# A decoder trunk on one core: a new address raster for the operand pools, the second scale matrix on VectorE, and the last probabilities product placed earlier

## The chip, the core and the metric

The kernel runs on one core of a Trainium2 chip, as one launch. The metric is the device time of that launch in microseconds (us). The kernel before takes 2453.76 us (median of three runs, 2452.49 to 2454.29). Differences of 0.2% and less, about 4.9 us here, cannot be told from no change.

## What is computed

Two decoder layers over 1024 tokens of width 1024, all in float32. The layers differ in their mixer; the rest is the same:

```python
h = x
for layer in range(2):
    hn = rmsnorm(h, g_mix[layer])
    # layer 0: gated convolution + gMLP gating; layer 1: latent attention (8 heads) + mLSTM (4 heads)
    mix = even_mixer(hn, ...) if layer % 2 == 0 else odd_mixer(hn, positions, ...)
    h = h + mix                                  # mix ends in a 1024 x 1024 output projection
    h = h + swiglu(rmsnorm(h, g_ffn[layer]), w_gate[layer], w_up[layer], w_down[layer])   # D_FF = 2816
    gate = sigmoid(rmsnorm(h, g_ple[layer]) @ w_ple_gate[layer])
    h = h + gate * (p[layer] @ w_ple_proj[layer])
```

Attention is causal softmax over blocks of 128 queries; each head's output is the product of its probabilities with V, and the heads are concatenated before the output projection.

## The kernel before

**Products.** The work is held transposed: tiles of 128 partitions by 512 columns, two token halves `n` of 512 tokens, eight feature blocks `k` of 128. A float32 operand is kept as two fp32r tiles, a high part made on ScalarE (`split`, L146) and the remainder made on VectorE (L147), with the letters `h` and `l` in their names (`xch`, `xcl`; `hu`, `lu`). One product of 128x128 by 128x512 is three matmuls, high by high, low by high and high by low (`mm3`, L189 to L191). In the rows a matmul reads `out<-moving,stationary`: `p<-xch,hu` streams `xch` past the weights `hu`. The stationary operand of the next matmul is loaded (PEld) while the matmul before it streams.

**Where tiles lie.** Pools are stacked in each partition's memory in the order in which they are opened: constants; `opB` (32 slots of 2 KB); `w`, which holds six tiles with the tag `raw` (weights as they come from memory, 2 KB each), eight `whi` and eight `wlo` (the split weights); `tmp` (working tiles, some of them 2056 bytes or a few bytes long); and last `opA` (the slots from number 32 up), which the attention's own pools replace during attention. A slot below 32 is in `opB`, one from 32 up in `opA`. With the sizes of the program, `opB`, `raw`, `whi` and `wlo` all begin at 832 bytes past a multiple of 2048 (`opB` at byte 19264, `whi` at 97088, `wlo` ends at 129856), and `opA` begins at byte 151488, which is 1984 past a multiple of 2048. Taken modulo 256 that is 64 for the first group and 192 for `opA`. "Raster" below means this remainder.

**Which products use which pool.** Layer 0's input projection reads the normalised input from the `x0` tiles, which lie in `opA` (slots 32 to 63); its weights are the `w` tiles. SwiGLU's gate and up projections are done by a seven-product scheme on quarters of the operands: for each of 22 column units and each layer, 7 products of 4 operand pairs, each pair one `mm3`. The operand tiles of products 1 and 2 (`xb`) and 4 lie in `opB`; those of the rest (`xc`) are placed as they are made, in the order 6, 7, 5, 4, 3, by

```python
free = iter(list(range(32, 54)) + list(range(16, 32)) + [54, 55])
```

so that products 6 and 7 lie in `opA` wholly, of product 5 three pairs in four, and of product 3 one pair in four: 12 of the 28 pairs. The gate projection at the layer's end (`ppg`) keeps the first token half in `opB` and the second in `opA`; its projection of `p` (`ppj`) has its tokens `pT` in `opA`, and at the end of layer 1 its weights `wj` too.

**Row scales.** `bcast_prep` splits a row vector of scales in two and puts each part on the diagonals of a 128x512 matrix, `dg`; `bcast` multiplies both with a matrix of ones (`Rb`, L298 and L299) so that the scales stand in all partitions, and ScalarE copies the sum out. This happens ten times in the program.

**The end of attention.** A loop over 64 pairs of head and query block transposes probabilities (`PT`, L1875), has ScalarE copy them out (`PTs`, L1877) and multiplies them with V (`O<-V,PTs`, L1833) one step later: `lag` holds the product that is still to be done. After a head's last product `head_done` divides by the row sums (`yp`, L1815), and after a pair of heads `pair_out` transposes the pair's output for a token half (`yaT`, L1824) and splits it (`y1h`, `y1l`), from where it is an operand of the output projection. The two `pair_out` calls of the last pair wait in `todo`. Behind the loop the output projection is begun: two output blocks `ot`, each of seven operand pairs (21 matmuls `po`); the eighth pair is the one that the last heads make. The engines run their instructions in the order in which the program issues them; a scheduler of the compiler moves a few neighbours.

Of the kernel before, what the change touches and what calls it, by code (L numbers as in the profile page):

```python
# [11 lines left out]
F32 = mybir.dt.float32  # L12
# [9 lines left out]
P = 128  # L22
# [4 lines left out]
HT = 512  # L27
# [12 lines left out]
RAW = 6  # L40
# [6 lines left out]
class Build:  # L47
# [59 lines left out]

    def w_part(self, srcs, kt, cols, name, gcol, slots=None):
        nc = self.nc
        raw = self.wp.tile([P, kt, cols], F32, tag="raw", name=self.name(f"r{name}"), bufs=RAW)  # L110
        o = 0
        for s in srcs:
            w = s.shape[1]
            nc.sync.dma_start(raw[:, :, o : o + w], s.rearrange("(k p) c -> p k c", p=P))
            o += w
        if gcol is not None and kt > 1:
            g = self.vec[:, gcol : gcol + kt].unsqueeze(2).to_broadcast([P, kt, cols])
            nc.gpsimd.tensor_tensor(out=raw, in0=raw, in1=g, op=ALU.mult)
        if slots:
            hi, lo = (  # L120
                self.slot(i, name=f"u{name}").rearrange("p (k c) -> p k c", k=kt) for i in slots
            )
        else:
            hi = self.wp.tile([P, kt, cols], F32R, tag="whi", name=self.name(f"h{name}"), bufs=8)
            lo = self.wp.tile([P, kt, cols], F32R, tag="wlo", name=self.name(f"l{name}"), bufs=8)
        if gcol is not None and kt == 1:
            self.split_scaled(hi, lo, raw, self.vec[:, gcol : gcol + 1])
        else:
            self.split(hi, lo, raw)
        return [(hi[:, k, :], lo[:, k, :]) for k in range(kt)]  # L130
# [23 lines left out]

    def w_quarter(self, w, rows, c, name):

        t = self.wp.tile([P, 4, P], F32, tag="raw", name=self.name(f"r{name}"), bufs=RAW)
        self.nc.sync.dma_start(
            t, w[rows * HT : (rows + 1) * HT, c].rearrange("(k p) c -> p k c", p=P)
        )  # L160
        return t
# [7 lines left out]
    def w_chain(self, w, c0, c1, name, eng):  # L169


        tt = eng.tensor_tensor
        raw = lambda: self.wp.tile([P, 4, P], F32, tag="raw", name=self.name(f"s{name}"), bufs=RAW)
        a11 = self.w_quarter(w, 0, c0, name)
        a21 = self.w_quarter(w, 0, c1, name)
        a22 = self.w_quarter(w, 1, c1, name)
        a12 = self.w_quarter(w, 1, c0, name)
        s1, s2 = raw(), raw()
        tt(out=s1, in0=a21, in1=a22, op=ALU.add)
        tt(out=s2, in0=s1, in1=a11, op=ALU.subtract)  # L180
        tt(out=a21, in0=a11, in1=a21, op=ALU.subtract)
        return {1: a11, 2: a12, 4: a22, 5: s1, 6: s2, 7: a21}
# [95 lines left out]
    def bcast_prep(self, r):  # L278

        nc = self.nc  # L280
        rh = self.tp.tile([P, 4], F32R, tag="rh", name=self.name("rh"), bufs=2)
        rl = self.small("rl", (P, 4))
        nc.vector.tensor_copy(rh, r)
        nc.vector.tensor_tensor(out=rl, in0=r, in1=rh.bitcast(F32), op=ALU.subtract)
        out = []
        for i, x in enumerate((rh.bitcast(F32), rl)):
            d = self.tmp("dg", (P, 4, P), F32R)
            (nc.vector, nc.gpsimd)[i].tensor_tensor(
                out=d, in0=self.ident.unsqueeze(1).to_broadcast([P, 4, P]),
                in1=x.unsqueeze(2).to_broadcast([P, 4, P]), op=ALU.mult,  # L290
            )
            out.append(d.rearrange("p a b -> p (a b)"))
        return out
# [31 lines left out]
def trunk(ctx, tc, x, p, positions, g_mix, g_ffn, g_ple, ev_w_in, ev_w_conv, ev_g_v, ev_w_s,  # L325
          ev_b_s, ev_w_out, od_w_in, od_b_gate, od_g_qa, od_g_kva, od_w_q_up, od_w_kv_up, od_g_q,
          od_g_k, od_g_mh, od_w_out, w_gate, w_up, w_down, w_ple_proj, w_ple_gate, out):
    nc = tc.nc
    B = Build(tc)
    x = x[0]  # L330
# [3 lines left out]
    bp = ctx.enter_context(tc.tile_pool(name="opB", bufs=1))  # L334
    dp = ctx.enter_context(tc.tile_pool(name="dram", bufs=1, space=DRAM))
    B.wp = ctx.enter_context(tc.tile_pool(name="w", bufs=1))
    B.tp = ctx.enter_context(tc.tile_pool(name="tmp", bufs=1))

    def open_ps():
        s = ExitStack()  # L340
# [316 lines left out]
    def ffn_down(l, act_d, h_d, h2_d, X2, st, normed):  # L657
# [6 lines left out]

        def part(fh, ch, f, t=None):
            if t is None:
                t = B.wp.tile([P, HT], F32, tag="raw", name=B.name("rd"), bufs=RAW)
            r = (fh * half + f) * P
            nc.sync.dma_start(t, w_down[l][r : r + P, ch * HT : (ch + 1) * HT])
            return t  # L670
# [163 lines left out]
    def ple_out(l, tok, h2_d, X, r):  # L834

        pT = {}
        for n in range(2):
            pT[n] = make_pT(load_p(l, n) if n else tok, [32 + 4 * n + i for i in range(4)])
        for cg in range(2):
            c = slice(cg * HT, (cg + 1) * HT)  # L840
            grp = B.tm_load(w_ple_gate[l], [(cg * HT, (cg + 1) * HT)], f"pg{cg}")
            hs = {}
            for n in range(2):
                for j in range(4):
                    t = hs[n, j] = B.slot(n * 4 + j + 8 * cg, F32, "h2")
                    nc.sync.dma_start(t, h2_d[n][cg * 4 + j])
            wj = []
            for k in range(2):
                raw = B.wp.tile([P, HT], F32, tag="raw", name=B.name("rpj"), bufs=RAW)
                nc.sync.dma_start(raw, w_ple_proj[l][k * P : (k + 1) * P, c])  # L850
                a = B.slots2(40 + 4 * cg + 2 * k, 41 + 4 * cg + 2 * k, "wj")
                B.split(a[0], a[1], raw)
                wj.append(a)
            for tt in range(NT):
                n, t = tt // 4, slice((tt % 4) * P, (tt % 4 + 1) * P)
                pg = B.tm_mm(grp, X, tt, "ppg")
                pj = B.ps("ppj")
                for k in range(2):
                    a = pT[n][k]
                    B.mm3(pj, (a[0][:, t], a[1][:, t]), wj[k], k == 0, k == 1)  # L860
                ph = B.ps_tr("ph")
                for j in range(4):
                    nc.tensor.transpose(ph[:, j * P : (j + 1) * P], hs[n, j][:, t], ident)
                s = B.tmp("psg")
                nc.scalar.activation(s, pg, AF.Sigmoid, scale=r[n][:, tt % 4 : tt % 4 + 1])
                nc.vector.tensor_tensor(out=s, in0=pj, in1=s, op=ALU.mult)
                nc.vector.tensor_tensor(out=s, in0=ph, in1=s, op=ALU.add)
                nc.sync.dma_start(out[tt * P : (tt + 1) * P, c], s)
# [373 lines left out]
    def up_weights(src, kt, cols, gcol, name):  # L1242
        pairs = []
        half = cols // 2
        for k in range(kt):
# [2 lines left out]
            )  # L1248
            for i in range(2):
                c = slice(i * half, (i + 1) * half)  # L1250
                raw = B.wp.tile([P, half], F32, tag="raw", name=B.name(f"r{name}"), bufs=RAW)
                nc.sync.dma_start(raw, src[k * P : (k + 1) * P, c])
                B.split_scaled(t[0][:, c], t[1][:, c], raw, col(gcol + k))
            pairs.append(t)
# [634 lines left out]
    for ot in range(2):  # L1889
        u = B.w_unit(od_w_out[0][:, ot * P : (ot + 1) * P], KT, P, f"wo{ot}")  # L1890
        po = psum("S", "po", 4)
        for i, k in enumerate(order[:-1]):
            B.mm3(po, u[k], mixT[0][k], i == 0, False)
        begun[0, ot] = u, po
    run_lag()
    for fn in todo:
        fn()
    for _ in mem:
        pass
    at.close()  # L1900
# [44 lines left out]
```

## Time and profile before

| | |
|---|---|
| median of three runs | 2453.76 us |
| the profiled execution | 2453.51 us |
| its span, first to last instruction | 2451.8 us (so 1.7 us lie around it) |
| granted TensorE clock | 0.999 of full speed |
| TensorE matmul (PE) busy | 2413.6 us, 98% |
| VectorE (DVE) busy | 1561.2 us, 64% |
| ScalarE (ACT) busy | 988.2 us, 40% |
| GpSimd (POOL) busy | 679.8 us, 28% |
| DMA, hardware queue | 348.25 MB, 45.3% of 16 engines' span |

A share of busy time is a mean over stages, so each stage has to be read by itself: where PE is busy without a gap, only the rate at which matmuls follow each other can change the time; where another engine is full, PE's rate doesn't matter there.

### The profile page before, as it was taken

To read this page: it belongs to the slowest core of one execution; us is meant where nothing else is said; L and a number is where in the kernel's file an instruction comes from. 1 tells how busy PE (TensorE), PEld (TensorE's weight loads), DVE (VectorE), ACT (ScalarE), POOL (GpSimd) and SP (SyncE) were. 2 spreads that over 40 slices of the span, in tenths; PEclk is the share of its full clock that TensorE was granted. 3 is DMA by queue.
4 is the path that set the end of the run, shared out by engine and by line. 5 is a ranking of instruction groups with operands and counts; after the bars stand their busy time and mean duration, and the time that the engine had idled before them with its cause. 6 is when DMAs were issued, how large, how long until landed. Compare 5 with 4: busy or idle time off the path is not lost.

```text
span 2451.8 us, 33875 instructions
## 1 busy us (share of the span) xinstructions
PE 2413.6 (98%) x11510; PEld 1993.8 (81%) x11510; DVE 1561.2 (64%) x3079; ACT 988.2 (40%) x1877; POOL 679.8 (28%) x678
## 2 busy tenths in 40 slices
PE   7999999999999999999999999999999999999999
PEld 6878887788888888888888788878788888888877
DVE  6864479645556778776785566548855455687731
ACT  5322244233233545444554455635333232454520
POOL 3452121546553000112321132111256556100000
PEclk9999999999999999999999999999999999999999
DMA  4221453433236966553454843154433233886721
GB/s 151 78 86 48 136 169 101 141 99 112 91 108 204 308 226 214 174 173 96 114 154 121 228 112 106 46 168 134 129 120 112 87 111 103 286 281 210 251 97 39
DMA packets 358685, 350.74 MB, mean 143 GB/s; under 512 B 24011, under 2 KB 249648, under 8 KB 358512
## 3 DMA queue, kind: packets, MB, share of 16 engines
q1 hardware_dynamic: 358016, 348.25, 45.3%
q8 instruction: 90, 1.47, 0.2%
q0 software_dynamic: 464, 0.33, 0.1%
q14 instruction: 83, 0.68, 0.1%
q10 hardware_dynamic: 32, 0.01, 0.0%
HBM read 255.18 MB, written 93.32 MB: 142 GB/s over the span
## 4 chain that ended last, share of the span: by engine, by line
PE 52%; DVE 4%; issue 2%; DMA 1%; ACT 1%; POOL 0%; SPq 0%; DVEq 0%; POOLq 0%; ACTq 0%
PE p L190 5%; PE p L189 5%; PE p L191 5%; PE pd L189 3%; PE pd L190 3%; PE pd L191 3%; PE O L1833 2%; PE ppg L191 2%; PE ppg L190 2%; PE ppg L189 2%; PE PT L1875 1%; PE po L189 1%; PE po L190 1%; PE po L191 1%; PE S L1775 1%
## 5 line engine op out<-in xcount | busy, mean ns | idle before, releaser
L189 PE MATMUL pd<-acth,hd 128*128 128x512 f32 x616 | 240.0, 390 | 0.1
L190 PE MATMUL pd<-actl,hd 128*128 128x512 f32 x616 | 239.7, 389 | 0.0
L191 PE MATMUL pd<-acth,ld 128*128 128x512 f32 x616 | 239.7, 389 | 0.0
L189 PE MATMUL p<-xch,hg 128*128 128x512 f32 x440 | 173.1, 394 | 5.3 <-DVE sg L534 2.2
L190 PE MATMUL p<-xcl,hg 128*128 128x512 f32 x440 | 173.1, 393 | 0.2
L189 PE MATMUL p<-xch,hu 128*128 128x512 f32 x440 | 173.0, 393 | 0.0
L191 PE MATMUL p<-xch,lu 128*128 128x512 f32 x440 | 172.9, 393 | 0.0
L191 PE MATMUL p<-xch,lg 128*128 128x512 f32 x440 | 172.9, 393 | 0.0
L190 PE MATMUL p<-xcl,hu 128*128 128x512 f32 x440 | 172.6, 392 | 0.0
L541 POOL TENSOR_TENSOR act<-act,sg 128x512 f32<-128x512 f32 x60 | 90.0, 1499 | 244.1 <-DVE act L534 239.3
L146 ACT CAST hu<-ru 128x512 fp32r<-128x512 f32 x116 | 71.6, 622 | 183.3 <-PE p L190 170.4
L189 PEld LDWEIGHTS pd<-acth,hd 128*128 128x128 f32 x616 | 115.6, 188 | 24.3 <-DVE res L728 0.5
L191 PEld LDWEIGHTS pd<-acth,ld 128*128 128x128 f32 x616 | 115.6, 188 | 24.3
L146 ACT CAST hg<-rg 128x512 fp32r<-128x512 f32 x110 | 68.2, 620 | 165.9 <-PE p L190 135.6
L190 PEld LDWEIGHTS pd<-actl,hd 128*128 128x128 f32 x616 | 115.6, 188 | 23.8
L147 DVE TENSOR_TENSOR lu<-ru,hu 128x512 fp32r<-128x512 f32 x116 | 117.2, 1011 | 14.9 <-ACT hu L146 14.9
L146 ACT CAST hd<-rd 128x512 fp32r<-128x512 f32 x110 | 68.3, 621 | 133.5 <-PE pd L190 82.2
L147 DVE TENSOR_TENSOR actl<-ra,acth 128x512 fp32r<-128x512 f32 x154 | 109.5, 712 | 12.1 <-ACT acth L146 12.0
L259 POOL TENSOR_TENSOR S<-S,sq 128x512 f32<-128x512 f32 x38 | 51.6, 1359 | 219.7 <-ACT sq L257 219.7
L147 DVE TENSOR_TENSOR ld<-rd,hd 128x512 fp32r<-128x512 f32 x110 | 76.9, 699 | 47.6 <-ACT hd L146 47.6
L189 PEld LDWEIGHTS p<-xch,hg 128*128 128x128 f32 x440 | 82.6, 188 | 26.5 <-ACT hg L146 3.0
L146 ACT CAST acth<-ra 128x512 fp32r<-128x512 f32 x154 | 94.7, 616 | 13.1 <-DMA ra<-act 9.3
(561 smaller groups left out, 6615.9 us busy)
## 6 DMA issues: line engine op xcount, KB each, us to landing
ra<-act SPq DMA_DIRECT2D x154, 256.0 KB, 3.7
rd<-in_w_down SPq DMA_DIRECT2D x154, 256.0 KB, 4.0
rg<-in_w_gate SPq DMA_DIRECT2D x100, 256.0 KB, 3.3
ru<-in_w_up SPq DMA_DIRECT2D x100, 256.0 KB, 2.9
act<-act SPq DMA_DIRECT2D x88, 256.0 KB, 2.0
act<-at SPq DMA_DIRECT2D x66, 256.0 KB, 2.0
rpg<-in_w_ple_gate SPq DMA_DIRECT2D x48, 256.0 KB, 3.0
sd<-in_w_down SPq DMA_DIRECT2D x44, 256.0 KB, 4.2
```

The source lines that it names most:

```text
L146: self.nc.scalar.copy(hi, src)
L147: (eng or self.nc.vector).tensor_tensor(out=lo, in0=src, in1=hi.bitcast(F32), op=ALU.subtract)
L189: mm(ps, a[0], b[0], start=first, stop=False, skip_group_check=more)
L190: mm(ps, a[0], b[1], start=False, stop=False, skip_group_check=more)
L191: mm(ps, a[1], b[0], start=False, stop=last, skip_group_check=more)
L259: eng.tensor_tensor(out=st[n], in0=st[n], in1=sq, op=ALU.add)
L541: (nc.vector if last else nc.gpsimd).tensor_tensor(out=t, in0=t, in1=sg[d["i"], key], op=ALU.mult)
L1775: mm(s[:, 0:w], q0, K0[:, c0 : c0 + w], start=True, stop=False)
L1833: nc.tensor.matmul(O[h][:, b * DV : (b + 1) * DV], t[:, j * P : (j + 1) * P], V[h // 2][:, kb, (h % 2) * DV : (h % 2 + 1) * DV], start=kb ...
L1875: nc.tensor.transpose(pt[:, j * P : (j + 1) * P], e[:, j * P : (j + 1) * P], ident)
```

## The change

Three edits:

1. **Pools.** The `raw` tiles leave `w` for a pool of their own, and that pool and `tmp` are placed from the other end of the partition's memory. `opA` then follows directly behind `wlo`.
2. **Scale matrices.** Both `dg` matrices are made on VectorE; before, the second was made on GpSimd.
3. **Last head pair.** `run_lag()`, the last product of probabilities and V, is called ahead of the first output products, and the two `pair_out` calls between the two output blocks.

```diff
@@ w_part, w_quarter, w_chain, part, ple_out, ev: the same edit at each raw tile
-        raw = self.wp.tile([P, kt, cols], F32, tag="raw", name=self.name(f"r{name}"), bufs=RAW)
+        raw = self.rp.tile([P, kt, cols], F32, tag="raw", name=self.name(f"r{name}"), bufs=RAW)
...
@@ bcast_prep
-        for i, x in enumerate((rh.bitcast(F32), rl)):
+        for x in (rh.bitcast(F32), rl):
             d = self.tmp("dg", (P, 4, P), F32R)
-            (nc.vector, nc.gpsimd)[i].tensor_tensor(
+            nc.vector.tensor_tensor(
...
@@ trunk
     B.wp = ctx.enter_context(tc.tile_pool(name="w", bufs=1))
-    B.tp = ctx.enter_context(tc.tile_pool(name="tmp", bufs=1))
+    B.rp = ctx.enter_context(tc.tile_pool(name="raw", bufs=1, side="right"))
+    B.tp = ctx.enter_context(tc.tile_pool(name="tmp", bufs=1, side="right"))
...
@@ end of attention
         po = psum("S", "po", 4)
+        if ot == 0:
+            run_lag()
         for i, k in enumerate(order[:-1]):
             B.mm3(po, u[k], mixT[0][k], i == 0, False)
         begun[0, ot] = u, po
-    run_lag()
-    for fn in todo:
-        fn()
+        if ot == 0:
+            for fn in todo:
+                fn()
```

With the sizes of the program `whi` then begins at byte 84800, `wlo` at 101184 and `opA` at 117568, all 832 past a multiple of 2048, as `opB` still does: every matmul operand of these pools has the remainder 64 modulo 256. The `raw` tiles begin at byte 217056, which is 2016 past a multiple of 2048 and so 32 past a multiple of 64; before they were on a multiple of 64. Which tile is made when, and in which slot, is unchanged. The line numbers behind the edits grow by one to three (L1833 becomes L1834).

On TensorE, at the end of attention, the program before has the last probabilities product behind the second output block, with both transposes of the pair, the eighth operand's products (`y1h_2980`) and nothing else behind it:

```order
L191 MATMUL po_16089<-y1h_2978_13214,lwo_0_3763_16080 128x512
L1833 MATMUL O_15891<-V_15190,PTs_16039 128x64
L1824 MATMUL yaT_16116<-ident,yp_15882 128x128 x4
L189 MATMUL po_16055<-y1h_2980_13216,hwo_0_3755_16045 128x512
L189 MATMUL po_16089<-y1h_2980_13216,hwo_0_3762_16079 128x512
L1824 MATMUL yaT_16123<-ident,yp_15882 128x128 x4
L190 MATMUL po_16055<-y1l_2981_13217,hwo_0_3755_16045 128x512
```

After the change the product stands behind the first output block's third matmul, its first transposes behind that block's last, and the second transposes seven matmuls later:

```order
L191 MATMUL po_16058<-y1h_2982_13221,lwo_4_3759_16055 128x512
L1834 MATMUL O_15894<-V_15193,PTs_16042 128x64
L189 MATMUL po_16058<-y1h_2984_13223,hwo_4_3758_16054 128x512
...
L191 MATMUL po_16058<-y1h_2978_13217,lwo_0_3756_16049 128x512
L1825 MATMUL yaT_16085<-ident,yp_15885 128x128 x4
L189 MATMUL po_16111<-y1h_2982_13221,hwo_4_3768_16107 128x512
...
L189 MATMUL po_16111<-y1h_2986_13225,hwo_4_3768_16107 128x512
L1825 MATMUL yaT_16092<-ident,yp_15885 128x128 x4
```

What moved is `O`, and with it `yp` and `yaT`: 18 matmuls `po` now lie between `O` and the first `yaT`.

On VectorE, at the row scales of layer 0's SwiGLU (`rh` and `rl` are the two parts of the scales, `lu` the low part of a weight tile, `h` the residual that is scaled), before:

```order
L284 TENSOR_TENSOR rl_3272<-rt_3251,rh_3271 128x4
L288 TENSOR_TENSOR dg_3275<-ident,rh_3271 128x512
L147 TENSOR_TENSOR lu_3308<-ru_3305,hu_3307 128x512
L421 SCALAR_TENSOR_TENSOR h_2728<-h_2728,vec,R_3303 128x512
```

and after:

```order
L284 TENSOR_TENSOR rl_3275<-rt_3254,rh_3274 128x4
L288 TENSOR_TENSOR dg_3278<-ident,rh_3274 128x512
L288 TENSOR_TENSOR dg_3280<-ident,rl_3275 128x512
L147 TENSOR_TENSOR lu_3311<-ru_3308,hu_3310 128x512
L422 SCALAR_TENSOR_TENSOR h_2731<-h_2731,vec,R_3306 128x512
```

The second `dg` comes from GpSimd's list, where nothing else changes place, and stands directly behind the first; so it is at all ten places.

## Rows read from the trace of the kernel before

**Rows 1.** The page's first part: busy time of each engine, its share of the span, and its instructions.

```profile
PE 2413.6 (98%) x11510; PEld 1993.8 (81%) x11510; DVE 1561.2 (64%) x3079; ACT 988.2 (40%) x1877; POOL 679.8 (28%) x678
```

**Rows 2.** What TensorE waited for, over the whole span: the line that waited, what it waited for, microseconds in total, how often, the longest.

```profile
PE zv L189 <- ACT x0h L146: 4.0, 1, 4.0
...
PE Rb L299 <- POOL dg L288: 1.5, 4, 0.4
```

**Rows 3.** Busy time of each engine in a stretch of the span (first column, us), with the number of its instructions; the column behind the engines is the granted clock, then the DMA engines' busy share and GB/s. The first stretch is in layer 0's down projection, the second in its input projection; the next two are the beginnings of SwiGLU in layers 0 and 1; the last is layer 1's down projection.

```profile
800.00:900.00 100.00, 100.00 (x442) 82.82 (x442) 75.36 (x123) 51.06 (x92) 0.00 (x0) 1.00 0.82 273
145.00:245.00 100.00, 100.00 (x432) 81.07 (x431) 45.59 (x62) 19.50 (x31) 31.39 (x28) 1.00 0.19 56
361.00:432.00 71.00, 68.50 (x293) 54.13 (x291) 70.06 (x108) 33.72 (x58) 14.05 (x8) 1.00 0.32 100
1690.00:1759.00 69.00, 66.66 (x284) 52.86 (x284) 67.76 (x102) 32.35 (x55) 12.89 (x8) 1.00 0.32 100
2112.00:2325.00 213.00, 212.94 (x946) 176.08 (x945) 166.79 (x275) 102.98 (x183) 6.31 (x4) 1.00 0.77 255
```

**Rows 4.** The timeline of TensorE in SwiGLU of layer 0: start, duration, line, operands. Up to 449.31 the `xch` tiles are those in `opB`, from there on those in `opA`; ten matmuls are left out at each "...".

```profile
446.81 0.39 PE L190 MATMUL p<-xcl,hu 128*128 128x512 f32 x1
...
449.31 0.40 PE L189 MATMUL p<-xch,hu 128*128 128x512 f32 x1
...
451.87 0.39 PE L191 MATMUL p<-xch,lg 128*128 128x512 f32 x1
```

**Rows 5.** The timeline of TensorE at the end of layer 1. In `ppj<-wjh,pTh` both operands lie in `opA`; in `ppg<-hpg,xph` at this place the stationary `xph` is in `opA` and the moving weights in `w`. Three matmuls are left out at the first "...", nine at the last.

```profile
2357.22 0.39 PE L190 MATMUL ppj<-wjl,pTh 128*128 128x512 f32 x1
...
2358.12 0.40 PE L191 MATMUL ppj<-wjh,pTl 128*128 128x512 f32 x1
...
2359.03 0.39 PE L190 MATMUL ppg<-lpg,xph 128*128 128x512 f32 x1
...
2361.35 0.39 PE L191 MATMUL ppg<-hpg,xpl 128*128 128x512 f32 x1
```

**Rows 6.** Groups of TensorE's instructions by line, operands and shape over the whole span: busy time, mean ns of one, idle time before them and who ended it. Each product has its three lines; one line of each is shown.

```profile
L191 PE MATMUL p<-xch,lg 128*128 128x512 f32 x440 | 172.9, 393 | 0.0
...
L189 PE MATMUL ppg<-xph,hpg 128*128 128x512 f32 x128 | 50.4, 394 | 0.0
...
L191 PE MATMUL px<-x0h,lx 128*128 128x512 f32 x64 | 25.3, 395 | 0.0
...
L189 PE MATMUL pu<-x0h,hu 128*128 128x512 f32 x48 | 19.0, 395 | 0.0
...
L191 PE MATMUL zv<-hzva,x0l 128*128 128x512 f32 x32 | 13.2, 412 | 0.0
...
L190 PE MATMUL ppj<-pTl,hpj 128*128 128x512 f32 x32 | 12.7, 397 | 0.0
```

**Rows 7.** The timeline of all engines at the end of attention; a bracket is the idle time of that engine before the instruction and what ended it.

```profile
1589.96 0.27 ACT L1877 COPY PTs<-PT 128x128 f32<-128x128 f32 x1 [0.37 <-PE PT L1875]
1590.11 0.48 PE L191 MATMUL po<-y1h,lwo 128*128 128x512 f32 x1
...
1599.09 0.39 PE L191 MATMUL po<-y1h,lwo 128*128 128x512 f32 x1
...
1599.68 0.69 DVE L1815 TENSOR_TENSOR yp<-O,rr 128x512 f32<-128x512 f32 x1 [1.09 <-PE O L1833]
...
1600.43 0.65 PE L1824 MATMUL yaT<-ident,yp 128*128 128x128 f32 x4 [0.79 <-DVE yp L1815]
...
1601.74 0.69 DVE L147 TENSOR_TENSOR y1l<-yaT,y1h 128x512 fp32r<-128x512 f32 x1 [1.36 <-ACT y1h L146]
...
1601.76 0.73 PE L189 MATMUL po<-y1h,hwo 128*128 128x512 f32 x2 [0.68 <-ACT y1h L146]
...
1602.48 0.66 PE L1824 MATMUL yaT<-ident,yp 128*128 128x128 f32 x4
...
1603.90 0.40 PE L189 MATMUL po<-y1h,hwo 128*128 128x512 f32 x1
```

**Rows 8.** The timeline at two of the ten row scales: first that of layer 0's SwiGLU, then, two rows, TensorE at one ahead of it. The last row is the group of all ten matrices made on GpSimd: shortest, median and longest duration in ns, and first and last start.

```profile
361.86 0.68 DVE L288 TENSOR_TENSOR dg<-ident,rh 128x512 fp32r<-128x512 f32 x1
...
362.02 1.42 POOL L288 TENSOR_TENSOR dg<-ident,rl 128x512 fp32r<-128x512 f32 x1 [9.31 <-DVE rl L284]
...
362.46 1.53 DVE L147 TENSOR_TENSOR lu<-ru,hu 128x512 fp32r<-128x512 f32 x1
...
362.60 0.49 PE L298 MATMUL Rb<-dg,ones 128*128 128x512 f32 x1
...
363.49 0.50 PE L299 MATMUL Rb<-dg,ones 128*128 128x512 f32 x1 [0.40 <-POOL dg L288]
...
321.54 0.40 PE L298 MATMUL Rb<-dg,ones 128*128 128x512 f32 x1
322.01 0.50 PE L299 MATMUL Rb<-dg,ones 128*128 128x512 f32 x1
...
L288 POOL TENSOR_TENSOR dg<-ident,rl x10: 1279/1367/1422, 28.2 to 1688.8; 128x512 fp32r<-128x512 f32 x10
```

**Rows 9.** Two loads of 128 KB. First the times from issue to landing of the loads of `mkT`, whose tile begins 32 bytes past a multiple of 64 in the attention's pool; then the group of the loads of `rzK`, a `raw` tile on a multiple of 64: kind and number, size, median us from issue to landing.

```profile
DMA to landing us min/median/max: 2.6/2.7/4.9
...
rzK<-in_od_w_in SPq DMA_DIRECT2D x8, 128.0 KB, 2.6
```

More of the change, by code (lines that the diff above doesn't have):

```diff
@@ L155, in w_quarter @@
     def w_quarter(self, w, rows, c, name):
-        t = self.wp.tile([P, 4, P], F32, tag="raw", name=self.name(f"r{name}"), bufs=RAW)
+        t = self.rp.tile([P, 4, P], F32, tag="raw", name=self.name(f"r{name}"), bufs=RAW)
         self.nc.sync.dma_start(
@@ L172, in w_chain @@
         tt = eng.tensor_tensor
-        raw = lambda: self.wp.tile([P, 4, P], F32, tag="raw", name=self.name(f"s{name}"), bufs=RAW)
+        raw = lambda: self.rp.tile([P, 4, P], F32, tag="raw", name=self.name(f"s{name}"), bufs=RAW)
         a11 = self.w_quarter(w, 0, c0, name)
@@ L666, in part @@
             if t is None:
-                t = B.wp.tile([P, HT], F32, tag="raw", name=B.name("rd"), bufs=RAW)
+                t = B.rp.tile([P, HT], F32, tag="raw", name=B.name("rd"), bufs=RAW)
             r = (fh * half + f) * P
@@ L848, in ple_out @@
             for k in range(2):
-                raw = B.wp.tile([P, HT], F32, tag="raw", name=B.name("rpj"), bufs=RAW)
+                raw = B.rp.tile([P, HT], F32, tag="raw", name=B.name("rpj"), bufs=RAW)
                 nc.sync.dma_start(raw, w_ple_proj[l][k * P : (k + 1) * P, c])
@@ L1250, in up_weights @@
                 c = slice(i * half, (i + 1) * half)
-                raw = B.wp.tile([P, half], F32, tag="raw", name=B.name(f"r{name}"), bufs=RAW)
+                raw = B.rp.tile([P, half], F32, tag="raw", name=B.name(f"r{name}"), bufs=RAW)
                 nc.sync.dma_start(raw, src[k * P : (k + 1) * P, c])
```

## The prediction

> **What bounds the kernel now.** I read the page's first part, then what TensorE waited for, then stretches, then the timeline matmul by matmul. TensorE is busy for 98% of the span, the others for 64% at most [rows 1], and the longest of its waits are single waits of a few us [rows 2]. So in most stages nothing but the rate at which matmuls follow each other sets the time. The reader should look at that rate in two stretches of 100 us, both without an idle moment and both at the full granted clock: 442 matmuls in one, 432 in the other [rows 3], nearly all of the same shape. That is 226.2 ns from start to start in the first and 231.5 ns in the second: 5.3 ns apart. Two short stretches elsewhere are exceptions: there VectorE is busy 70.06 of 71 us and 67.76 of 69 us while TensorE is idle for 2.5 and 2.3 us [rows 3]; VectorE bounds these.
>
> What tells the fast stretch from the slow one is seen where one group of matmuls turns into another with no change in shape, weights pool or engine load. In layer 0's SwiGLU eleven steps take 2.50 us (227 ns) as long as `xch` lies in `opB`, and the next eleven take 2.56 us (233 ns), when it lies in `opA` [rows 4]. At the end of layer 1, with weights and tokens both in `opA`, four steps take 0.90 us (225 ns); with the one in `opA` and the other in `w`, ten steps take 2.32 us (232 ns) [rows 5]. So neither `opA` nor `w` is slow by itself; slow is the pair of a streaming operand in the one and the next weights in the other. By the layout that is where the two differ in raster (192 against 64 modulo 256).
>
> **The raster.** The change puts `opA` on the raster of `opB` and `w`. I count the matmuls of 512 columns that have one operand in `opA` and the other in `w` or `opB` [rows 6] (the numbers behind the x; each product has three lines). Layer 0's input projection: three outputs like `px` with 3x64 each, `pu` with 3x48 and a further 3x16 beside it, and `zv` with 6x32: 576+192+192 = 960. SwiGLU: 12 pairs of 28 x 3 matmuls x 22 units x 2 layers = 1584. The gate projections: `ppg` has 128 in each of six lines, and its second token half, half of these 768, is 384; `ppj` with weights in `w` has 3x32 = 96. In all 3024. At 5.3 ns each [rows 3] that is 16.0 us, at the 5.5 ns of [rows 4] 16.6 us.
>
> Not all of it comes out. In the two stretches bounded by VectorE, 293+284 = 577 matmuls run [rows 3]; by the share of 12 in 28 some 247 of them would gain, 1.3 us in all, and VectorE keeps it. At the start, TensorE waits for the first `x0h` [rows 2] and for loads; I leave out 100 of the `zv` matmuls, 0.5 us. Net: 16.0 - 1.3 - 0.5 = **14.2 us**. The bounds are 0, if the raster isn't the cause, and 16.6, if nothing is absorbed.
>
> The Trainium skill speaks against this term: the page "TensorE: Matmul & The Clock Gate", in the section "Step-by-step: what each phase is for", says that TensorE has two independent read ports, one for the streaming operand and one for the weights, and that loading the next weights takes no read bandwidth from the matmul that runs. By that the two addresses could not matter and this term would be 0; the rows show a difference that goes with the pair of pools, so I hold to them, and price the rule as a rival.
>
> **The last head pair.** Before, the chain behind the first output products is bare: from the last `po` at 1599.09 to the first of the next block at 1603.90, 4.81 us [rows 7]. The work in it is 0.23 for that last `po`, one `O`, eight transposes at about 0.11 (an estimate: 0.66 for four [rows 7], of which the last one's way through the array is hidden by what follows) and six `po` at 0.227: 0.23 + 0.2 + 0.9 + 1.4 = 2.7. The rest is the wait for `yp` (0.79) and for `y1h` (0.68) and what TensorE needs to start again behind each [rows 7]: 2.1 us. After the change `O` stands behind the first block's third `po`, which started at 1590.11. Does it wait there? Its `PTs` is copied from 1589.96 to 1590.23 [rows 7], and the matmul behind that third `po` can't start before 1590.34, so no. `yp` is then ready about 1.1 us later (O ends, then 0.69), while its transposes stand 18 matmuls, 4.1 us, behind. The first transposes end, the cast and the remainder take 1601.08 to 1602.43 = 1.35 us [rows 7], and the second transposes, which use the same PSUM tile, stand 7 matmuls = 1.6 us behind: no wait again. So the 2.1 us go wholly, I take **2.0**; the bounds are 0 (a new wait for `PTs` or the PSUM tile of the same size) and 2.1. What is late next is nothing: the copies on ScalarE and VectorE have a mostly idle stretch there.
>
> **The scale matrices.** At four of the ten places TensorE waits for the GpSimd matrix, 1.5 us in total [rows 2]. At one of them the VectorE matrix starts at 361.86 and the next VectorE instruction at 362.46, so a matrix occupies VectorE for 0.60; the second one would start at 362.46 and end 0.68 later at 363.14, whereas GpSimd's ends at 362.02 + 1.42 = 363.44 [rows 8]. That is 0.30 earlier: 4 x 0.30 = 1.2. At two further places no wait is shown but the step between the two `Rb` is 0.47 (321.54 to 322.01) instead of one matmul's 0.23 [rows 8]; I expect 0.24 from each, 0.5 in all. The other four gain nothing. Cost: 0.60 of VectorE ten times. What is queued behind on VectorE is `lu`, and TensorE needs its weights. But `lu` takes 1.53 beside GpSimd's matrix [rows 8], where an instruction of that form takes 0.69 (`y1l`) [rows 7]: alone it would start at 363.06 and end at 363.75, ahead of the present 363.99. So the extra 0.60 is paid back by the end of the overlap, and GpSimd isn't waited for by anything there. Sum **1.7**; bounds -1 (the 0.60 counts in full in the two stretches that VectorE bounds) and 2.
>
> **Sum.** 14.2 + 2.0 + 1.7 = 17.9. The profiled execution took 2453.51, its span of 2451.8 and 1.7 around it; 2453.5 - 17.9 = 2435.6, so **2436**. The median of the runs, 2453.76, is 0.25 above the execution that was profiled; I make nothing of that.
>
> **Rivals.**
>
> *Not the raster but a place in memory.* Before, each slow pair also has one operand above and one below some point between 129,856 (end of `wlo`) and 151,488 (start of `opA`). It isn't distance: `opB` and `wlo` lie up to 110,000 bytes apart and are fast, `opA` and `wlo` are slow at 22,000. But a fixed boundary in that stretch, such as the middle 131,072, would fit all rows as well. Then only the slots of `opA` that now lie under it gain, about (131,072 - 117,568) / 2048 = 6.6 of its tiles; these hold product 6's first operands and some of `x0`, and I count 612 of the slow pairs: 612 x 5.3 = 3.2 us. Total 3.2 + 2.0 + 1.7 = 6.9, **2446.6**. For it speaks that nothing in the trace separates the two; against it, that the boundary would have to lie just in that 22 KB. Chance 0.13.
>
> *Addresses don't matter at all*, and the 5.3 ns come from something that goes with these stages otherwise. Then the raster gives 0 and the rest 3.7: **2449.8**. Against it: the step in the middle of one stage, at the very matmul where the pool changes [rows 4]. Chance 0.07. This is what the Trainium skill's rule of two independent read ports, cited above, would give.
>
> *Slower: the `raw` tiles.* They come to lie 32 bytes past a multiple of 64, and every weight is loaded into them. In the down projections the DMA engines are busy 0.77 of the time for 213 us [rows 3] (layer 0's is much the same). About half of what they move there are the weights' tiles. If a load into such a tile took f times as long, the engines would be full from 0.77 x (1 + (f-1)/2) = 1, f = 1.6; at f = 2 they would need 0.77 x 1.5 = 1.155, 33 us more in each layer's projection, 66 in all: 2436 + 66 = **2502**. Against it: the loads of `mkT`, to a tile that is likewise off, land in 2.6 to 2.7 us and those of `rzK`, to an aligned tile and of the same size, in 2.6 [rows 9]. Chance 0.04.
>
> **How the numbers follow.** My forecast, the raster with the other two, has a chance of 0.76 and by itself a range from 2432 (16.6 + 2.1 + 2.0 = 20.7) to 2441 (if a third of the raster's gain is absorbed elsewhere). The place in memory has 0.13, no effect of addresses 0.07, the slow loads 0.04. The range of 8 in 10 reaches to the place in memory: 2432 to 2447. 0.2% is 4.9 us: the first two cases are faster than that (0.89), the third is within it (a little of the second case too): faster 0.88, same 0.08, slower 0.04.
>
> **What would show it.** Raster: in 145 to 245 us, shifted by little, some 442 matmuls per 100 us instead of 432; the steps behind the change of `xch` from `opB` to `opA` at 227 ns; mean durations of `px` and `p<-xch` down from 393 and 395 [rows 6] to about 390. If only the first slots of `opA` become fast, it is a place in memory; if none, addresses aren't the cause. Last head pair: no wait of `yaT` for `yp` nor of `po` for `y1h`, and the two output blocks directly followed by the next. Scale matrices: no wait of `Rb`, steps of 0.23 to 0.6, `lu` at 0.7. Loads: the landing times of `rd` and the DMA share in the down projections; if they grow, the last rival is at work. The prediction is wrong if the 5.3 ns stay, or if VectorE's stretches grow by more than a microsecond.

## The result, and the profile after

The changed kernel takes 2432.21 us (median), the kernel before beside it 2453.69: a ratio of 0.9912, 95% interval 0.9895 to 0.9929, or 21.5 us less. In a later series it was 0.9908 (0.9895 to 0.9920). The prediction was 2436 in a range of 2432 to 2447, so the time lies at the very edge of the range; the direction and the mechanism held, and the gain was 3.6 us larger than the sum. The profiled execution took 2432.94, its span 2430.8, so the span is shorter by 21.0 us.

The page's first part, which answers to [rows 1]: TensorE's busy time fell by 18.4 us, nearly the whole gain, with the same work (eight matmuls lack a record in this trace, hence 11502 for 11510).

```profile
PE 2395.2 (99%) x11502; PEld 1995.5 (82%) x11510; DVE 1562.5 (64%) x3089; ACT 987.8 (41%) x1877; POOL 668.6 (28%) x668
```

Stretches, in the columns of [rows 3]: the input projection, the down projection, the beginnings of SwiGLU in layers 0 and 1, and four microseconds within the former.

```profile
145.00:245.00 100.00, 100.00 (x443) 82.82 (x442) 42.97 (x61) 19.98 (x31) 30.11 (x26) 1.00 0.18 53
800.00:900.00 100.00, 100.00 (x443) 82.82 (x442) 78.17 (x127) 50.15 (x90) 0.00 (x0) 1.00 0.81 266
361.00:432.00 71.00, 66.24 (x280) 53.13 (x280) 64.72 (x101) 31.97 (x54) 12.39 (x7) 0.98 0.37 115
1690.00:1759.00 69.00, 65.28 (x283) 52.25 (x282) 62.51 (x97) 28.19 (x47) 14.06 (x8) 1.00 0.41 127
...
424.00:428.00 4.00, 4.00 (x12) 3.13 (x11) 2.54 (x4) 1.49 (x3) 0.00 (x0) 0.57 0.63 206
```

The input projection now runs at the down projection's rate, 443 matmuls in 100 us where there were 432. The beginning of SwiGLU in layer 0 became worse: more idle time of TensorE than in [rows 3] (4.8 us, before 2.5), and a granted clock of 0.57 within it. The timeline at the place of [rows 4] has no step any more where `xch` passes from `opB` to `opA` (at 443.57): eleven matmuls take 2.49 us ahead of it and 2.50 us behind.

```profile
441.08 0.39 PE L190 MATMUL p<-xcl,hu 128*128 128x512 f32 x1
...
443.57 0.39 PE L189 MATMUL p<-xch,hu 128*128 128x512 f32 x1
...
446.07 0.39 PE L191 MATMUL p<-xch,lg 128*128 128x512 f32 x1
```

What TensorE waited for, in the columns of [rows 2]:

```profile
PE p L189 <- DVE u L595: 5.4, 2, 3.3
...
PE S L1776 <- DMA Q<-qTd: 3.4, 1, 3.4
PE zv L189 <- ACT x0h L146: 2.8, 1, 2.8
```

The same view of before has these three beside the two of [rows 2]:

```profile
PE p L189 <- DVE sg L534: 2.2, 2, 1.1
...
PE S L1775 <- DMA Q<-qTd: 1.7, 1, 1.7
...
PE p L189 <- DVE u L594: 1.7, 2, 0.9
```

`Rb` no longer waits for GpSimd, the wait for `x0h` is shorter, and that for `u` of VectorE has grown from 1.7 to 5.4 us.

Where the 21.0 us lie is seen by taking the same matmul in both traces and comparing its start. From one stretch of before to the next the lead grows by:

| stretch of before, us | what runs there | gain, us | the same in a second trace of the changed kernel ("All of it again", below) |
|---|---|---|---|
| 0 to 100 | first products, scale matrix | 2.2 | 2.8 |
| 100 to 300 | input projection, layer 0 | 4.8 | 2.4 |
| 300 to 400 | output projection, start of SwiGLU | 0.6 | 0.6 |
| 400 to 450 | SwiGLU bounded by VectorE | -1.8 | 0.6 |
| 450 to 800 | SwiGLU, layer 0 | 4.6 | 5.0 |
| 800 to 1000 | down projection, scale matrix | 0.7 | 0.4 |
| 1000 to 1150 | gate projection, layer 0 | 2.2 | 2.2 |
| 1150 to 1500 | attention up to the last heads | -1.8 | -1.0 |
| 1500 to 1650 | end of attention, output projection | 2.4 | 2.4 |
| 1650 to 1750 | start of SwiGLU, layer 1 | 0.8 | 0.7 |
| 1750 to 2100 | SwiGLU, layer 1 | 5.0 | 4.1 |
| 2100 to end | down and gate projection, layer 1 | 1.4 | 2.0 |

So single stretches differ by 2 us and more between two executions of one kernel. Part of that is the clock: the granted clock is 0.50 for 3.4 us at 129 us in the second of these traces and not in the first, and at 424 us in the first and not in the second. The loss in attention is one wait, of `S` for the load of `Q`: 3.4 us in after, 2.3 in the second trace, 1.7 before; over all traces it lies between 1.4 and 3.4, and no run shows what sets it.

### The profile page after: what moved, and what is told of

It reads as the page before. It is cut to its first block, busy times and chain, and to the rows that moved or that the text cites. A ratio compares the mean times of both kernels' runs of the same rounds, so it can differ in the third digit from the quotient of the medians.

```text
span 2430.8 us, 33858 instructions
## 1 busy us (share of the span) xinstructions
PE 2395.2 (99%) x11502; PEld 1995.5 (82%) x11510; DVE 1562.5 (64%) x3089; ACT 987.8 (41%) x1877; POOL 668.6 (28%) x668
## 4 chain that ended last, share of the span: by engine, by line
PE 86%; DVE 8%; DMA 3%; issue 1%; ACT 1%; POOL 0%; SPq 0%; DVEq 0%; ACTq 0%; POOLq 0%
PE p L190 10%; PE p L189 10%; PE p L191 10%; PE pd L189 6%; PE pd L190 6%; PE pd L191 6%; PE po L189 2%; PE po L191 2%; PE po L190 2%; PE O L1834 2%; PE ppg L191 2%; PE ppg L189 2%; PE ppg L190 2%; PE PT L1876 1%; PE S L1776 1%
```

## Experiments

Each run is set beside the kernel before on its own chip; a single execution of that kernel varies by some microseconds there, so the traces say more than the medians where an edit is worth two.

### The pools alone, and the rest alone

Edit of the first: after, with `bcast_prep` and the end of attention as before. Edit of the second: before, with these two edits and the old pools.

> The pool change alone: raw tiles and tmp from the other end, opA on the raster of opB and w; scale matrices and the last head pair as before. If the raster of opA against w is the cause: 14 us from it and up to 3 us more that the sum did not have, 2436 to 2440 us, and 443 matmuls in 145 to 245 us. If the unpredicted 3 us belong to the two other edits: 2439.5.

Measured: 2444.0 against 2455.8, ratio 0.9948 (0.9936 to 0.9960), 12.8 us (9.8 to 15.7). The 14 us of the sum are within that, but the median misses both times that were expected; the five runs spread from 2438 to 2446, and the one that was profiled, the fastest, leads before by 15.3 us. 442 matmuls in 145 to 245 us. Wait of `Rb` as before; up to 100 us nothing is gained (0.1 us).

> The two other edits without the pools. By the sum of the prediction 2.0 + 1.7 = 3.7 us: 2450.0. If the unpredicted 3 us are theirs: 2447. If they are worth nothing without the pools: 2453.7. TensorE shows no wait of Rb for dg, and none of yaT for yp.

Measured: 2448.0, ratio 0.9970 (0.9960 to 0.9980): 7.4 us, twice the 3.7 of the sum. In the trace 2.6 us of the 6.1 by which its span is shorter stand within the first 100 us. 432 matmuls in 145 to 245 us. The fast rate came with the pools alone, and the gain at the start, which the sum did not have, with the small edits alone.

### The raster or the place in memory

```diff
-    B.tp = ctx.enter_context(tc.tile_pool(name="tmp", bufs=1))
+    B.tp = ctx.enter_context(tc.tile_pool(name="tmp", bufs=1, side="right"))
```

> Before, with only tmp placed from the other end: raw stays in w on its old raster, and opA begins at byte 129856, directly behind wlo, 832 past a multiple of 2048. Raster theory: the slow step of opA against w goes as in the pool change, some 14 us less, 2438 to 2440. Place in memory (a boundary near 131072): the pairs lie on both sides of it as before, so nothing: 2453. If it is slower than the pool change alone by 2 to 3 us, the raw tiles' own raster is worth that.

Measured: 2442.1, ratio 0.9941 (0.9929 to 0.9953), as much as the whole pool change within the intervals (and slower than the 2438 to 2440 expected), with the pairs still on both sides of the byte 131,072. Its row of the stretch:

```profile
145.00:245.00 100.00, 100.00 (x443) 82.88 (x442) 43.83 (x61) 19.41 (x31) 31.40 (x27) 1.00 0.19 55
```

And the other way round, after with a difference of 128 bytes put back:

```diff
+    B.pad = ctx.enter_context(tc.tile_pool(name="pad", bufs=1))
     B.rp = ctx.enter_context(tc.tile_pool(name="raw", bufs=1, side="right"))
...
-    bb = cp.tile([P, NT, MH], F32, name="bb")
+    bb = B.pad.tile([P, NT, MH], F32, name="bb")
```

> After, with one constant tile of 128 bytes moved between w and opA: opB and w begin 128 bytes lower, opA stays, so the rasters differ by 128 as they did before, while nothing else changes place. Raster theory: the slow step comes back, 3024 x 5.3 less what is absorbed, +14 to +16: 2446 to 2448, and 432 matmuls in 145 to 245 us. If the gain came from anything else in the pool change: 2432.

Measured: 2450.7, ratio 0.9977 (0.9969 to 0.9986), 0.69% or 17 us slower than after by the two ratios to before (14 to 16 were expected), and the slow rate is back:

```profile
145.00:245.00 100.00, 100.00 (x432) 81.13 (x431) 42.70 (x59) 19.28 (x30) 30.26 (x26) 1.00 0.18 53
```

Raw tiles, `tmp` and `opA` lie in this run at the same bytes as in after. The place in memory is refuted by both, and so is that the gain came from the new home of the raw tiles.

### How large a difference costs how much

The same edit with other tiles: the 320-byte tile `vec`, the two 128-byte tiles `bb` and `dec`, and a tile of 32 bytes made for it.

> After, with the constant tile of 320 bytes moved between w and opA: the two rasters differ by 320 bytes, 64 modulo 256. In 145 to 245 us some 432 matmuls if any difference costs the same 5 to 6 ns; 443 if only a difference of 128 does.

> After, with two constant tiles of 128 bytes moved between w and opA: a difference of 256 bytes. If what counts is the remainder modulo 256, as the prediction had it: 443 matmuls in 145 to 245 us, as in the changed kernel. If it is the place in the 2048 bytes: 432.

> After, with a tile of 32 bytes put between w and opA: a difference of 32 bytes, and opA no longer on a multiple of 64. 432 matmuls in 145 to 245 us if every difference that is not a multiple of 256 costs the same; fewer if being off a multiple of 64 costs more, 443 if only a difference of 128 costs.

Measured, each in a single execution beside one of before at 2454.1: 2446.5, 2438.0 and 2450.9. The same stretch of the three, in this order:

```profile
145.00:245.00 100.00, 100.00 (x439) 82.05 (x438) 41.71 (x60) 19.25 (x30) 30.96 (x26) 1.00 0.19 53
```

```profile
145.00:245.00 100.00, 100.00 (x443) 82.80 (x442) 42.69 (x60) 19.26 (x30) 29.94 (x27) 1.00 0.19 53
```

```profile
145.00:245.00 100.00, 100.00 (x430) 80.34 (x429) 42.34 (x59) 19.25 (x30) 31.11 (x26) 1.00 0.19 53
```

256 bytes cost nothing in that stretch, so it is the remainder that counts, and the differences don't cost the same. The mean step from one matmul of 512 columns to the next (steps of 200 to 260 ns), by where the moving operand and the next weights lie:

| `opA` ahead of `w` by, modulo 256 | runs | moving in `opA`, next weights in `w`, ns | moving in `w`, next weights in `opA`, ns |
|---|---|---|---|
| 0 | after; 256 bytes | 226.8; 226.8 | 227.9; 227.9 |
| 32 | 32 bytes | 233.4 | 233.1 |
| 64 | 320 bytes | 229.7 | 233.2 |
| 128 | before; 128 bytes | 232.8; 232.7 | 232.4; 232.4 |

Each number is over 2,561 to 2,569 pairs in the one column and 349 to 359 in the other. At 64 the order matters: the moving operand 64 ahead of the weights costs 2.9 ns, the weights 64 ahead of the moving operand 5.3. The expectation for 320 bytes had two answers and missed the third; at 32 bytes the cost is nearly that of 128. That it is the next weights and not the present ones is argued from the loads, which overlap the matmul before; in these stages both lie in the same pool, and no run separates them.

### The scale matrices alone

```diff
-            (nc.vector, nc.gpsimd)[i].tensor_tensor(
+            nc.vector.tensor_tensor(
```

> Before, with the second scale matrix on VectorE as the only edit. The prediction's sum: -1.7 us. Theory from the run of both small edits: GpSimd's matrix at 28 us delays GpSimd's next instructions, for which VectorE waits, and that chain ends in the x0h for which TensorE waits at 48 us: 2.5 us more, -4.2 us in all, with the wait of zv for x0h down from 4.0 to about 2.0 us. Rival: the 2.5 us came from when the first loads landed; then -1.7 us, and the wait of zv at about 4 us.

Measured: 2450.4 against 2456.9, ratio 0.9979 (0.9971 to 0.9988), 2.9 to 7.1 us: the 1.7 us of the prediction's sum lie outside, the 4.2 within. TensorE's wait is 3.0 us, between the two answers:

```profile
PE zv L189 <- ACT x0h L146: 3.0, 1, 3.0
```

The mechanism begins in the first 40 us. Before, GpSimd's timeline has the matrix ahead of the sums `gvs` for which VectorE waits, and then the scaling of weights, `ru`:

```profile
28.17 1.35 POOL L288 TENSOR_TENSOR dg<-ident,rl 128x512 fp32r<-128x512 f32 x1 [0.83 <-DVE rl L284]
29.49 1.03 POOL L939 TENSOR_TENSOR gvs<-gv 128x512 f32<-128x512 f32 x1
31.38 1.04 POOL L939 TENSOR_TENSOR gvs<-gv 128x512 f32<-128x512 f32 x1 [0.86 <-DVE v L941]
32.38 4.04 POOL L118 TENSOR_TENSOR ru<-ru,vec 128x512 f32<-128x512 f32 x4
```

In the run `gvs` starts 0.90 us earlier:

```profile
28.59 1.15 POOL L939 TENSOR_TENSOR gvs<-gv 128x512 f32<-128x512 f32 x1 [0.97 <-ACT gv L934]
30.42 1.04 POOL L939 TENSOR_TENSOR gvs<-gv 128x512 f32<-128x512 f32 x1 [0.69 <-PE xT L882]
```

VectorE's chain behind `gvs` feeds ScalarE's `vh`, and `x0h` stands behind these on ScalarE's list; it is cast 1.28 us earlier in the run (the second row) than before (the first):

```profile
51.67 1.06 ACT L146 CAST x0h<-xT 128x512 fp32r<-128x512 f32 x2
```

```profile
50.39 1.06 ACT L146 CAST x0h<-xT 128x512 fp32r<-128x512 f32 x2
```

The chain consists of instructions on 128x8 that take 0.17 us alone and, beside GpSimd's `ru`, as long as one of these (before):

```profile
32.48 0.96 DVE L236 TENSOR_SCALAR rqy<-rqy 128x8 int32<-128x8 int32 x1
33.48 0.96 DVE L240 SCALAR_TENSOR_TENSOR rqw<-rqy 128x8 f32<-128x8 f32 x1
...
39.82 0.17 DVE L243 TENSOR_TENSOR rqw<-rqw,v 128x8 f32<-128x8 f32 x1
```

So what GpSimd starts later, VectorE ends later. The Trainium skill (page "SBUF — State Buffer", section "SBUF: two separate sides") states that the two share a pair of ports, which a GpSimd instruction, or a VectorE one with two inputs or in a two-port mode, holds for its whole length. These rows agree, with 0.96 for the small instruction and 1.01 for one `ru`; in which mode the first row's instruction, of one input, runs is not shown.

Over all traces the wait of `zv` for `x0h` is 3.7 to 4.0 us in the four kernels with the matrix on GpSimd (before, the pools alone, `tmp` on the other end, the last head pair alone) and 2.0 to 3.0 in the nine traces with it on VectorE, 2.5 in the mean: some 1.3 us are the edit's, not the 2.5 of the expectation. The lead at 100 us is 0 to 1.2 us in the four, 0.5 in the mean, and 0.7 to 2.9 in the nine, 2.2 in the mean. It scatters with how long TensorE's clock stays at its lower level near this wait: in 50 to 55 us the granted clock is 0.70 before and in this run, 1.00 in the run of both small edits, 0.50 in after.

### The last head pair alone

Edit: before, with the third part of the change.

> Before, with the order at the end of attention as the only edit: -2.0 us by the prediction's sum, all of it between 1590 and 1604 us of the trace; 0 if a new wait takes the place of the old ones.

Measured: 2453.9 against 2456.9, ratio 0.9991 (0.9982 to 0.9999), which can't tell 2.0 from 0.2. The trace can: the lead over before is constant from 1535 to 1590 us of before, and 2.05 us larger behind the first `po` of the third output block; in after by the same measure 2.1. But the profiled execution lost 4.7 us at 1524 to 1531 us of before, where after and the pool run lost none; the row of this stretch, then that of before:

```profile
1500.00:1535.00 35.00, 34.20 (x229) 30.42 (x229) 19.73 (x58) 18.05 (x52) 6.44 (x14) 0.85 0.28 78
```

```profile
1500.00:1535.00 35.00, 34.21 (x266) 30.05 (x264) 21.73 (x65) 21.25 (x62) 8.51 (x20) 1.00 0.33 90
```

The granted clock was 0.85 in it (0.50 for 10.2 us), and the only wait ahead of the fall, 0.8 us for `W`, is in the other traces too. The run with `tmp` on the other side shows the same there, and it shares no edit with this one. So two of thirteen executions have this loss, its cause isn't shown, and it alone is more than this edit is worth.

### All of it again, and the wait that it made

> The changed kernel again, beside its parts on one chip. If the parts add: the pools alone (-11.8 us of 2455.8 by the medians) and the two other edits without the pools (-7.7 us) make -19.5. If they share a gain, such as the waits of the first 60 us, less: -17.

Measured: 2433.2 against 2456.9, ratio 0.9908 (0.9895 to 0.9920), 23.7 us; the parts' ratios add to 0.82% (20 us), this is 0.92%. Within the intervals they add; of a shared gain, which would have made the whole less than the parts, there is no sign.

In after the longer wait for `u` has its cause in VectorE's list (timeline; a bracket is idle time and what ended it):

```profile
419.27 1.79 DVE L179 TENSOR_TENSOR sg<-rg,rg 128x512 f32<-128x512 f32 x1 [2.52 <-DMA rg<-in_w_gate]
421.09 1.64 DVE L181 TENSOR_TENSOR rg<-rg,rg 128x512 f32<-128x512 f32 x1
422.65 0.68 DVE L595 TENSOR_TENSOR u<-p,p 128x512 f32<-128x512 f32 x1
```

TensorE, faster by the raster, asks for `u` earlier, but `u` stands behind two sums of weights that wait for a load. The raster alone is enough for it: the five traces with these sums on VectorE and one raster wait 4.1 to 5.4 us for `u`, the seven with `opA` off 1.6 to 2.0. In this execution TensorE then starts again and, a microsecond later, runs at half its clock for eight matmuls, 0.43 us apart in place of 0.23:

```profile
423.47 0.47 PE L189 MATMUL p<-xch,hg 128*128 128x512 f32 x1 [3.27 <-DVE u L595]
...
424.48 0.63 PE L190 MATMUL p<-xcl,hg 128*128 128x512 f32 x1
...
427.89 0.39 PE L189 MATMUL p<-xch,hg 128*128 128x512 f32 x1
```

The fall of the clock is this execution's, not the kernel's: in the second trace the wait is 2.05 us here, and the clock stays up:

```profile
424.00 0.47 PE L189 MATMUL p<-xch,hg 128*128 128x512 f32 x1 [2.05 <-DVE u L595]
```

```profile
420.00:430.00 10.00, 7.80 (x34) 5.87 (x33) 8.75 (x10) 2.41 (x5) 4.39 (x3) 1.00 0.73 233
```

A version that takes these sums out of VectorE's way:

```diff
-                eng = nc.vector if d in ahead + third else nc.gpsimd
+                eng = nc.vector if d in ahead else nc.gpsimd
```

> After, with one line more: the weight sums of SwiGLU's third column unit are made on GpSimd, no longer on VectorE. In the trace of after VectorE stands 2.52 us at 416.7 us for a load that such a sum needs, then takes 1.79 and 1.64 us for two of them, and the u for which TensorE waits 3.27 us is queued behind; TensorE's clock then falls to half for 3.6 us (8 matmuls, some 1.6 us). If that queue is the cause: the waits of p for u (5.4 us in both layers) fall below 2 us, the clock stays up, 4 to 6 us less than after, about 2428. Rival: the load itself is late and the matmuls need its weights soon after, so the wait only moves to these: within 1 us of after, 2432 to 2434. On the other side, GpSimd's slower sums make the weights late: 2435 and more.

Measured: 2428.5 against 2455.8, ratio 0.9891 (0.9874 to 0.9909). The wait for `u` is gone in both layers, TensorE is busy without a gap there at the full clock:

```profile
400.00:424.00 24.00, 24.00 (x107) 19.88 (x106) 22.02 (x34) 7.79 (x13) 10.50 (x6) 1.00 0.44 134
420.00:440.00 20.00, 20.00 (x90) 16.57 (x89) 10.24 (x14) 5.19 (x9) 14.22 (x11) 1.00 0.61 199
```

Between 400 and 450 us of before the trace gains 5.2 us over the first trace of after and 2.7 over the second; between 1700 and 1770, 2.7 and 3.6. So the queue was the cause of the wait. Of the time, the intervals of after and of this version overlap; the two stretches of the trace are what shows the gain.

## Why the prediction was right, point by point

**The sum.** The time fell 0.2 us inside the range, and that is partly luck, since errors of the sum cancel. In the first trace the raster is worth 15.6 us where 14.2 were forecast, the last head pair 2.1 where it was 2.0, the scale matrices 5.0 where it was 1.7, and 1.8 are lost in attention, which the sum did not have: 20.9 against 17.9. The term that was mis-sized most is that of the scale matrices.

**The raster: right in kind, 14.2 us by the sum.** Both the undoing and the doing by another route move the rate, and no other edit brought it to 442 or 443. From the table, with the stretches of the input, SwiGLU and gate projections: 4.8 + 4.6 + 2.2 + 5.0 + 1.4 = 18.0, less the 1.8 lost at 400 to 450 and some 0.6 of a scale matrix at 1012: 15.6. The second trace gives 15.7 by the same stretches. Mean durations fell as forecast, `px` from 395 to 389 ns and `p<-xch` from some 393 to some 391. Two terms were mis-sized. The step was taken as 5.3 ns from two stretches; over the 2,971 pairs of the trace with one operand in `opA` it is 232.73 - 226.96 = 5.8 ns, 17.4 us for the 3024 that were counted. And the pairs that were on one raster all along got faster too: 227.35 to 226.93 ns over 5,800 pairs, 2.4 us, which the sum did not have (below, in the last section). On the other side the absorption was put at 1.3 us for the two stretches that VectorE bounds. In layer 0 the longer wait for `u` and the fall of the clock behind it took 1.8 us more than that stretch's gain in the first trace, while the second, without the fall, gained 0.6. The prediction had named a growth of VectorE's stretches by more than a microsecond as a sign of being wrong: in the first trace it came, in the second not. That a faster TensorE would meet VectorE's queue there is the step that the absorption left out.

One reading was thin: that the pair with both operands in `opA` is fast rested on four steps of 225 ns [rows 5]. Over all 76 such pairs the mean is 229.4 ns before and 226.8 after, so both in `opA` was not as fast as both on the other raster. The 128 bytes put back carry the point without it.

**The last head pair: right.** 2.0 forecast, 2.1 in the trace. `yp` is ready 3.3 us ahead of its transposes, and the second transposes start 0.1 us after the first remainder has ended, without a wait:

```profile
1578.95 0.33 PE L1834 MATMUL O<-V,PTs 128*128 128x64 f32 x2
...
1579.31 0.69 DVE L1816 TENSOR_TENSOR yp<-O,rr 128x512 f32<-128x512 f32 x1 [4.51 <-PE O L1834]
...
1583.28 0.60 PE L1825 MATMUL yaT<-ident,yp 128*128 128x128 f32 x4
...
1584.53 0.69 DVE L147 TENSOR_TENSOR y1l<-yaT,y1h 128x512 fp32r<-128x512 f32 x1 [1.98 <-ACT y1h L146]
1585.34 0.60 PE L1825 MATMUL yaT<-ident,yp 128*128 128x128 f32 x4
```

**The scale matrices: 1.7 forecast, about 4.5.** At the places of [rows 8] the order of events is as worked out: the second `Rb` stands 0.60 behind the first (355.31 and 355.91) where it was 0.89, and `lu` takes 0.69 in place of 1.53. But the six places that were counted give 2.8 us and not 1.7: in the run of this edit alone the lead over before grows there by 0.4 to 0.7 where `Rb` waited and by 0.3 at the two others; 0.3 and 0.24 were forecast for each.

```profile
355.17 0.69 DVE L288 TENSOR_TENSOR dg<-ident,rl 128x512 fp32r<-128x512 f32 x1
...
355.31 0.51 PE L298 MATMUL Rb<-dg,ones 128*128 128x512 f32 x1
...
355.77 0.69 DVE L147 TENSOR_TENSOR lu<-ru,hu 128x512 fp32r<-128x512 f32 x1
...
355.91 0.51 PE L299 MATMUL Rb<-dg,ones 128*128 128x512 f32 x1
```

One step failed outright: "The other four gain nothing", with its reason that GpSimd isn't waited for by anything there. That was looked at where `Rb` waits, not at every place where the matrix is made. At 28 us GpSimd's next instruction is `gvs`, VectorE waits for it, and its chain ends in the `x0h` for which TensorE waits longest; [rows 2] had that wait in its first line, and it was taken for one that the change doesn't touch. The wait is 1.3 us shorter in the mean over the runs, the lead at 100 us 1.7 larger; with the 2.8 that makes 4.5, within the 2.9 to 7.1 that the run of this edit alone measured.

**The rivals.** The place in memory fell by the run with `tmp` on the other side. That addresses don't matter, which the Trainium skill's rule of two independent read ports would give (page "TensorE: Matmul & The Clock Gate", section "Step-by-step: what each phase is for"), fell by the 128 bytes put back: the rule may hold for the ports, the rate it does not give. The raw tiles off their multiple of 64 cost nothing: the loads of `rd`, one of the largest groups, land as before. This row is of after,

```profile
DMA to landing us min/median/max: 2.5/4.0/6.9
```

and the same query on before gives the same three numbers.

## What to carry to other kernels

Where TensorE is busy without a gap, compare the matmul rate between stretches that do the same work: 2% between two of them was a matter of where two pools begin. Put the moving operands and the weights on one remainder modulo 256, and look again at it whenever a small tile is added to a pool between them. And before an instruction is taken off an engine, look at what stands behind it on both engines at every place where it occurs; a faster TensorE also comes earlier to the next queue, and there its gain can end.

## What the runs showed of the hardware

The cost of a matmul of 128x512 in fp32r, start to start, depends on the addresses of its moving operand and the weights modulo 256, and on which of the two is ahead: 226.8 to 227.9 ns at no difference, 229.7 with the moving operand 64 ahead, 232 to 234 at the other differences tried (the table above). Why these values, no run here shows.

Other engines matter as well, which I had not expected. The steps of `p<-xb` before are all on one raster. Counting an engine that is at work for at least half of the step, their mean is 230.8 ns for the 134 beside all three of VectorE, ScalarE and GpSimd, 230.6 for the 45 beside ScalarE and GpSimd, 229.6 for the 30 beside ScalarE alone, 227.7 for the 219 beside VectorE and ScalarE, and 226.7 for the 162 beside GpSimd alone. In after the first two classes have 226.7 (136) and 226.8 (44). At this place ScalarE writes weights into `w` and GpSimd works on tiles of `opA` and on `raw` tiles; so the raster of what other engines read and write seems to count too. All thirteen traces agree in it (227.4 to 228.0 ns for all pairs on one raster in the seven kernels with `opA` off, 226.9 in the six with it on), but no run was made that changes these engines' tiles alone.

TensorE's clock does not answer the same wait in the same way each time. In the five traces with one raster and the sums on VectorE, TensorE waits 2.0 to 3.3 us for `u` at ten places; within about a microsecond of its start again the clock fell to the lower level (0.50 granted, 1.2 GHz) for 3.4 us at five of them, and not at the other five. The longest two, 3.27 us in layer 0 of after and 3.32 us in layer 1 of the second trace, were followed by a fall and by none. In the seven traces with `opA` off the waits at this place, 0.8 to 1.1 us, were followed by none.
